# A hybrid mLSTM / gated-delta block on one core: when the z gate jobs enter the instruction streams, and three small moves around them

## The chip, the cores and the metric

The kernel runs on one core of a Trainium2 chip. The metric is the device time of one execution in microseconds (us). TensorE (PE) multiplies, VectorE (DVE) and ScalarE (ACT) do elementwise work, GpSimd (POOL) issues some of the DMAs and does some scaling, and SyncE (SP) issues most of the DMAs.

## The reference

The layer mixes two branches and then applies a feed-forward part, for 256 tokens and 2048 channels, in float32. Cut to what matters here:

```python
h = rms_norm(x, norm_mix_w) * (1 + scale_m) + shift_m
proj = h @ w_in                      # q, k, v, gates of both branches, merge gates
# branch B, 16 heads: gated delta rule; each chunk needs the inverse of a
# unit lower triangular matrix  a_mat = I + beta * (k k^T) * decay
o_b = rms_norm(gated_delta_both_directions(...), gdn_norm_w)
y_b = (o_b * silu(b_z)) @ w_branch_b          # b_z is the "z" gate
x = x + gate_m * ((g_a * y_a + g_b * y_b) @ w_out)     # stage o
hf = rms_norm(x, norm_ffn_w) * (1 + scale_f) + shift_f
x = x + gate_f * ((silu(hf @ w_gate) * (hf @ w_up)) @ w_down)
return rms_norm(x, norm_final_w)
```

## The kernel before

**Jobs.** Nearly every weight matrix is read once, in 1 MB pieces (a tile `raw_*`, loaded by SP). Each piece is cut into two halves, and each half is split into a high part `wh` (ScalarE, a copy that rounds) and a low part `wl` (VectorE, raw minus `wh`, line 211). TensorE then runs three products, high by high, high by low, low by high (lines 230 to 232), so a half of a job made by `tjob` costs 12 matmuls of 128x512. `raw`, `wh` and `wl` have three buffers each, so VectorE can be at most three halves ahead of TensorE. A job is a Python generator that gives out one half per step; the list `fills` holds the waiting jobs, and `fill(n)` takes n steps from its head.

**The 16 heads of branch B.** They go in four groups of four (g = 0 to 3). `gdn_phase1(h)` prepares a head: it ends with VectorE writing the tile `mi` from the product `ks`, and with GpSimd sending 32x32 blocks of `mi` to DRAM (`inst_d`, four DMAs), loading the decay factors `al` of head h+2 (`decay_load`, a memset and a 256 KB broadcast), and reading the blocks back as rows of the tile `uu` (line 657). When the four heads of a group are there, `gdn_invert(g)` solves the triangular blocks in `uu`: a memset (line 684) and 60 short VectorE operations in a chain (lines 689 and 695), and GpSimd stores the result (`inv_d`). `gdn_blocks(g)` loads it back (`cg`) and makes the tile `R`, which the first product of `gdn_phase2`, `p` (line 746), needs. While VectorE solves, `fill` gives TensorE projection jobs. The first of them is `z_job(g + 1)`, the z gate of the next group: four pieces, eight halves, 96 matmuls (`acc_z`).

**What sets the order.** Each engine runs its own queue in order. A scheduler writes the queues from the program, and may move instructions among each other; those wrapped in `order(...)` with a true second argument (or none) keep the program's order. In `tjob`, `early` is both the number of halves prepared before the first matmul and the argument that keeps the job's `wh` and `wl` instructions in program order:

```python
            order(S.activation(wh, raws[u][:, k0 : k0 + 2], AF.Copy), early)
            settle()
            order(V.tensor_tensor(wl, raws[u][:, k0 : k0 + 2], wh.bitcast(F32), ALU.subtract), early)
```

The z job of groups 1 to 3 is made with `early` = 1, near the end of the second `gdn_phase2` of a group.

**Behind stage o.** The last column block of stage o ends in three parts: token tile 0, then the left and right half of token tile 1 (`last_o`). VectorE multiplies by the gate row `gm` (`tm`, line 1199), adds to `x1` (line 1200), ScalarE squares and sums, and from the sums come the two scales `rs1` per token tile. ScalarE, VectorE and GpSimd then scale `x1` to `xn`; TensorE transposes `xn` (`pxn`) and the feed-forward part starts with the job `gt0` (`acc_gt`). GpSimd makes `xn` 1 to 3 (line 1252); `xn` 0 is made by the others.

**The end.** The last sums of stage d are followed by four scalings of 128x512 and four stores per token tile, all issued by SP (line 1416).

Of the kernel before, what the change touches and what calls it, by code (L numbers as in the profile page):

```python
# [11 lines left out]
AF = mybir.ActivationFunctionType  # L12
ALU = mybir.AluOpType
# [4 lines left out]
D = 2048  # L18
# [3 lines left out]
NH_B, DK_B = 16, 128  # L22
# [3 lines left out]
GRP = 4  # L26
# [26 lines left out]
def hybrid_block(ctx: ExitStack, tc: tile.TileContext, xr, nfr, crow, pk_d, cst_d, ada2, ada4, win0, winb, wint, wba, wbb, wo, wgu, wd, out, dbg=None):  # L53
    nc = tc.nc
    V, S, G, PE = nc.vector, nc.scalar, nc.gpsimd, nc.tensor
# [15 lines left out]
    def order(ins, yes=True):  # L71

        return tc.keep_in_program_order(ins) if yes else ins
# [189 lines left out]
    fills = []  # L263
# [34 lines left out]
    heads, parts = {}, {}  # L298
# [11 lines left out]
    def decay_load(h):  # L310
        al = als[h] = fr.tile([P, 2, T + 8], F32, tag="al", bufs=2, name=f"al{h}")
        order(G.memset(al[:, :, 0:8], 0.0))
        order(G.dma_start(al[:, :, 8:], alpha_d[:, h].partition_broadcast(P)))
# [48 lines left out]
    def z_job(g, early=0):  # L362
        def done(ps):
            szs[g] = evp.tile([P, 2, 512], F32, tag="sz", bufs=1, name=f"sz{g}")
            for t in range(2):
                S.activation(szs[g][:, t], ps[t], AF.Silu)
        return tjob(f"z{g}", [wint[g, u] for u in range(4)], hh, hl, done, early)
# [121 lines left out]
    with ExitStack() as s0:  # L489
# [3 lines left out]
        ss = w0.tile([P, 2], F32, name="ssx")  # L493
# [68 lines left out]
        zj = z_job(0, 3)  # L562
# [20 lines left out]
    def gdn_phase1(h):  # L583
# [13 lines left out]
        sq = fr.tile([P, 2, T], F32, tag="sqkq", bufs=1, name=f"sqkq{h}")  # L597
# [48 lines left out]
        g, hl_ = divmod(h, GRP)  # L646
# [5 lines left out]
                inst[4 * b : 4 * b + 4].rearrange("x j i -> j x i"), mi[32 * b : 32 * b + 32, :, 32 * b : 32 * b + 32]  # L652
            ), b)

        if h + 2 < NH_B:
            decay_load(h + 2)
        order(G.dma_start(uus[g][16 * hl_ : 16 * hl_ + 16], inst))

        cc = ccs[h % NB]

# [350 lines left out]
    for g in range(4):  # L1011
        blocks = gdn_blocks(g)
        next(blocks)
        fill(8)
        next(blocks)
        fill(1)
        pairs = [gdn_phase2(g, p) for p in range(2)]
        if g == 3:
            settle()
            sf.close()  # L1020
            mq["pool"] = pool(sq_, "mq", side="right")
            first2 = [mlstm(h) for h in range(2)]
            for c in first2:
                next(c)
        every[0] = (4, 2, 2, 2)[g]
        for p in range(2):
            pieces = stream(4 * g + 2 * p + 4)
            for n in range(1, 10):

                held[0] = n < 4  # L1030
                if p == 0:
                    next(blocks, None)
                if n == 9 and p and g < 3:

                    zj = z_job(g + 1, int(4 * g + 7 in heads))
                    if 4 * g + 7 in heads:
                        next(zj)
                next(pairs[p], None)
                if g == 3 and n == (8, 4)[p]:
                    next(first2[p])  # L1040
                for _ in range(last[n] if g == 3 else second[n] if p else after[n]):
                    next(pieces)
            for _ in pairs[p]:
                pass

            if g < 3:
                while 4 * g + 2 * p + 5 not in heads:
                    next(pieces)
        if g < 3:
            fills.insert(0, zj)  # L1050
            every[0] = owed[0] = 0
            if asked:
                add()
            invert(g + 1)
# [96 lines left out]
    gm = room[0][0].tile([P, D], F32, name="gm")  # L1151
# [38 lines left out]
    wp = pool(sw, "wp")  # L1190
    x1 = xp.tile([P, 2, D], F32, name="x1")
    S.dma_start(x1, xr)

    def residual(t, g, ps, gate, ss, rp, hold=False, part=slice(0, 512), acc=None, new=slice(0, 512)):

        c = slice(g * 512 + part.start, g * 512 + part.stop)
        n = slice(g * 512 + new.start, g * 512 + new.stop)
        tm = rp.tile([P, 512], F32, tag="tm", bufs=2, name=f"tm{ss.name}_{t}_{g}_{part.start}")
        order(V.tensor_tensor(tm[:, part], ps[:, : part.stop - part.start], gate[:, c], ALU.mult), hold)
        order(V.tensor_tensor(x1[:, t, c], x1[:, t, c], tm[:, part], ALU.add), hold)  # L1200
        order(S.activation(tm[:, new], x1[:, t, n], AF.Square, accum_out=ss[:, t, g : g + 1] if acc is None else acc), hold)

# [6 lines left out]
        order(V.tensor_reduce(rs[:, 3:5], ss[:, :, 0:3], mybir.AxisListType.X, ALU.add))  # L1209
        order(V.tensor_scalar(rs[:, 3:5], rs[:, 3:5], 1.0 / D, EPS, ALU.mult, ALU.add))  # L1210

    def token_root(rs, t):

        order(S.activation(rs[:, t : t + 1], rs[:, 5 + t : 6 + t], AF.Sqrt, bias=rs[:, 3 + t : 4 + t], scale=1.0 / D))

    def token_rstd(rs, t):
        order(V.reciprocal(rs[:, t : t + 1], rs[:, t : t + 1]))

    ss1 = xp.tile([P, 2, 4], F32, name="ss1")
    rs1 = xp.tile([P, 8], F32, name="rs1")  # L1220
# [26 lines left out]
    def normed(q, t, parts, eng):  # L1247
        if q not in xns:
            xns[q] = hp.tile([P, 2, 512], F32, tag="sg", bufs=2, name=f"xn{q}")
        o, i = xns[q][:, t, parts], x1[:, t, q * 512 + parts.start : q * 512 + parts.stop]  # L1250
        if eng is G:
            G.tensor_scalar(o, i, rs1[:, t : t + 1], None, ALU.mult)
        elif eng is V:
            order(V.tensor_scalar(o, i, rs1[:, t : t + 1], None, ALU.mult))
        else:
            order(S.activation(o, i, AF.Copy, scale=rs1[:, t : t + 1]))
# [3 lines left out]
    def last_o(t, ps, part):  # L1260

        sq = rs1[:, 5 + t : 6 + t]
        if not t:
            residual(0, 3, ps, gm, ss1, wp, True, acc=sq)
            token_root(rs1, 0)
        elif part == left:
            residual(1, 3, ps, gm, ss1, wp, True, acc=sq, new=left)
            order(V.scalar_tensor_tensor(rs1[:, 4:5], sq, 1.0 / D, rs1[:, 4:5], ALU.mult, ALU.add))
            token_rstd(rs1, 0)
            normed(0, 0, left, S)  # L1270
        else:
            residual(1, 3, ps, gm, ss1, wp, True, part, sq, part)
            token_root(rs1, 1)
            token_rstd(rs1, 1)

    def front_o():
# [73 lines left out]
    normed(0, 1, left, V)  # L1350
    for t in range(2):
        normed(0, t, right, S)
    for b in range(2):
        scaled, high = block(b)
        scaled()
        high()
# [44 lines left out]
    def finish(t):  # L1401

        token_root(rs2, t)
        token_rstd(rs2, t)
        r = rs2[:, t : t + 1]
        for g in (2, 0, 3, 1):
            o = x1[:, t, g * 512 : (g + 1) * 512]
            if g == 3:
                order(V.scalar_tensor_tensor(o, o, r, nf[:, 3 * 512 :], ALU.mult, ALU.mult))
            elif g == 2:  # L1410
                order(V.tensor_scalar(o, o, r, None, ALU.mult))
            else:
                order(S.activation(o, o, AF.Copy, scale=r))
        for g in (2, 0, 3, 1):
            c = slice(g * 512, (g + 1) * 512)
            order(nc.sync.dma_start(out[:, t, c], x1[:, t, c]))

    def front_d():
        means(ss2, rs2)
# [2 lines left out]
    for g in range(4):  # L1422
        c = slice(g * 512, (g + 1) * 512)
# [114 lines left out]
```

## Time and profile before

| | us |
|---|---|
| median of 3 runs (lowest, highest) | 2067.28 (2060.01, 2068.92) |
| the profiled execution | 2064.07 |
| its span, first to last instruction | 2062.1 |
| PE busy in the span | 2019.9 (98%) |
| VectorE busy | 1397.8 (68%) |
| ScalarE busy | 1027.7 (50%) |
| GpSimd busy | 116.8 (6%) |

The span lies 2.0 us under the time of its own execution. In rows of instructions the columns are start, duration, engine, line, operation, output<-inputs, shape and count; a bracket gives the idle time of the engine before the row and what ended it. Equal rows that follow each other are merged, with their count. A start is in us from the span's start. In rows of stretches each engine has its busy time and its count of instructions, then come the granted TensorE clock as a share of full speed, the busy share of the DMA engines and GB/s.

### The profile page before, as it was taken

To read this page: it belongs to the slowest core of one execution; us is meant where nothing else is said; L and a number is where in the kernel's file an instruction comes from. 1 tells how busy PE (TensorE), PEld (TensorE's weight loads), DVE (VectorE), ACT (ScalarE), POOL (GpSimd) and SP (SyncE) were. 2 spreads that over 40 slices of the span, in tenths; PEclk is the share of its full clock that TensorE was granted. 3 is DMA by queue.
4 is the path that set the end of the run, shared out by engine and by line. 5 is a ranking of instruction groups with operands and counts; after the bars stand their busy time and mean duration, and the time that the engine had idled before them with its cause. 6 is when DMAs were issued, how large, how long until landed. Compare 5 with 4: busy or idle time off the path is not lost.

```text
span 2062.1 us, 27024 instructions
## 1 busy us (share of the span) xinstructions
PE 2019.9 (98%) x10386; PEld 1697.9 (82%) x10386; DVE 1397.8 (68%) x2062; ACT 1027.7 (50%) x1540; POOL 116.8 (6%) x211
## 2 busy tenths in 40 slices
PE   8999999999999999999999999999999999999998
PEld 6878789978997889789787888788888888878886
DVE  5778877867878788866577778756565655455554
ACT  3146647755665577454534444644444444444443
POOL 0001210111001010110100000200000000000000
PEclk9999999999999999999999999999999999999999
DMA  9986666646666767586776878466766665555553
GB/s 401 420 334 208 193 228 225 215 124 218 227 206 207 241 213 244 189 291 250 258 278 249 321 283 296 157 232 232 255 225 226 251 237 184 187 201 191 197 189 137
DMA packets 78962, 485.64 MB, mean 236 GB/s; under 512 B 10585, under 2 KB 15969, under 8 KB 24433
## 3 DMA queue, kind: packets, MB, share of 16 engines
q1 hardware_dynamic: 63360, 450.95, 60.4%
q0 software_dynamic: 8160, 17.88, 4.0%
q10 hardware_dynamic: 7314, 15.10, 1.9%
q8 instruction: 81, 1.33, 0.3%
q14 instruction: 47, 0.39, 0.1%
HBM read 467.07 MB, written 16.82 MB: 235 GB/s over the span
## 4 chain that ended last, share of the span: by engine, by line
PE 85%; DMA 6%; DVE 6%; ACT 1%; issue 1%; POOL 0%; ACTq 0%; SPq 0%; DVEq 0%; POOLq 0%
PE acc_gt L230 4%; PE acc_gt L232 4%; PE acc_gt L231 4%; PE acc_up L232 4%; PE acc_up L230 4%; PE acc_up L231 4%; PE acc_d L231 4%; PE acc_d L230 4%; PE acc_d L232 4%; DMA ra<-ada 3%; PE acc_o L230 3%; PE acc_o L232 3%; PE acc_o L231 3%; PE acc_b L187 2%; PE acc_b L188 2%; PE acc_b L189 2%
## 5 line engine op out<-in xcount | busy, mean ns | idle before, releaser
L211 DVE TENSOR_TENSOR wl_d<-raw_d,wh_d 128x1024 fp32r<-128x1024 f32 x88 | 107.8, 1225 | 119.9 <-ACT wh_d L209 119.9
L211 DVE TENSOR_TENSOR wl_up<-raw_up,wh_up 128x1024 fp32r<-128x1024 f32 x88 | 107.7, 1225 | 111.3 <-ACT wh_up L209 111.2
L211 DVE TENSOR_TENSOR wl_gt<-raw_gt,wh_gt 128x1024 fp32r<-128x1024 f32 x88 | 108.1, 1229 | 89.2 <-ACT wh_gt L209 89.2
L187 PE MATMUL acc_b<-hh,wh_b 128*128 128x256 f32 x576 | 164.8, 286 | 0.0
L209 ACT ACTIVATE wh_d<-raw_d 128x1024 fp32r<-128x1024 f32 x88 | 93.3, 1061 | 138.9 <-PE acc_d L231 134.0
L189 PE MATMUL acc_b<-hh,wl_b 128*128 128x256 f32 x576 | 160.9, 279 | 0.0
L188 PE MATMUL acc_b<-hl,wh_b 128*128 128x256 f32 x576 | 159.7, 277 | 0.0
L209 ACT ACTIVATE wh_gt<-raw_gt 128x1024 fp32r<-128x1024 f32 x88 | 93.3, 1060 | 128.7 <-PE acc_gt L231 77.3
L111 DVE SCALAR_TENSOR_TENSOR ada<-ada,crow 128x2048 f32<-128x2048 f32 x64 | 146.1, 2282 | 10.2 <-DMA ada<-ada 10.2
L209 ACT ACTIVATE wh_up<-raw_up 128x1024 fp32r<-128x1024 f32 x88 | 93.2, 1060 | 118.1 <-PE acc_up L231 84.2
L230 PE MATMUL acc_gt<-wh_gt,hfh 128*128 128x512 f32 x352 | 139.0, 395 | 0.0
L231 PE MATMUL acc_gt<-wh_gt,hfl 128*128 128x512 f32 x352 | 138.2, 393 | 0.0
L232 PE MATMUL acc_gt<-wl_gt,hfh 128*128 128x512 f32 x352 | 137.4, 390 | 0.0
L230 PE MATMUL acc_up<-wh_up,hfh 128*128 128x512 f32 x352 | 136.9, 389 | 0.0
L231 PE MATMUL acc_up<-wh_up,hfl 128*128 128x512 f32 x352 | 136.9, 389 | 0.0
L232 PE MATMUL acc_up<-wl_up,hfh 128*128 128x512 f32 x352 | 136.9, 389 | 0.0
L230 PE MATMUL acc_d<-wh_d,ffh 128*128 128x512 f32 x344 | 134.3, 391 | 0.0
L231 PE MATMUL acc_d<-wh_d,ffl 128*128 128x512 f32 x344 | 134.3, 390 | 0.0
L232 PE MATMUL acc_d<-wl_d,ffh 128*128 128x512 f32 x344 | 133.9, 389 | 0.0
L557 PE MATMUL first<-x,raw 128*128 128x256 f32 x512 | 115.9, 386 | 6.3 <-ACT x L551 6.3
L557 PEld LDWEIGHTS first<-x,raw 128*128 128x128 f32 x512 | 97.3, 192 | 25.0 <-ACT x L551 11.9
L187 PEld LDWEIGHTS acc_b<-hh,wh_b 128*128 128x128 f32 x576 | 108.5, 188 | 1.2 <-issue 0.9
(373 smaller groups left out, 5261.3 us busy)
## 6 DMA issues: line engine op xcount, KB each, us to landing
ada<-ada SPq DMA_DIRECT2D x64, 1024.0 KB, 5.0
raw_gt<-wgu SPq DMA_DIRECT2D x44, 1024.0 KB, 4.9
raw_up<-wgu SPq DMA_DIRECT2D x44, 1024.0 KB, 4.9
raw_d<-wd SPq DMA_DIRECT2D x44, 1024.0 KB, 4.8
raw_b<-winb SPq DMA_DIRECT2D x36, 1024.0 KB, 5.1
ra<-ada SPq DMA_DIRECT2D x32, 1025.0 KB, 15.2
raw<-win SPq DMA_DIRECT2D x16, 1024.0 KB, 14.5
raw_z<-wint SPq DMA_DIRECT2D x16, 1024.0 KB, 5.4
```

What stands on the lines that cost most here:

```text
L111: order(V.scalar_tensor_tensor(raw, raw, 1.0, row_c[:, :D], ALU.mult, ALU.mult, accum_out=mod[:, c : c + 1]), room[0][3] > 1)
L187: PE.matmul(o, wh[:, k], hh[:, kk], start=kk == 0, stop=False)
L188: PE.matmul(o, wh[:, k], hl[:, kk], start=False, stop=False)
L189: PE.matmul(o, wl[:, k], hh[:, kk], start=False, stop=kk == KB - 1)
L209: order(S.activation(wh, raws[u][:, k0 : k0 + 2], AF.Copy), early)
L211: order(V.tensor_tensor(wl, raws[u][:, k0 : k0 + 2], wh.bitcast(F32), ALU.subtract), early)
L230: order(PE.matmul(ps[t], xh[:, kk, c], wh[:, k], start=kk == 0, stop=False), early and steps > 1)
L231: PE.matmul(ps[t], xl[:, kk, c], wh[:, k], start=False, stop=False)
L232: PE.matmul(ps[t], xh[:, kk, c], wl[:, k], start=False, stop=kk == last)
L557: PE.matmul(first[o], raw[:, o], x[:, b], start=b == 0 and o % 2 == 0, stop=b == KB - 1 and o % 2 == 1)
```

## The change

Five edits, all shown in the diff:

```diff
-        if h + 2 < NH_B:
+        final = hl_ == GRP - 1
+        if h + 2 < NH_B and not final:
             decay_load(h + 2)
         order(G.dma_start(uus[g][16 * hl_ : 16 * hl_ + 16], inst))
+        if h + 2 < NH_B and final:
+            decay_load(h + 2)
...
-                if n == 9 and p and g < 3:
-
-                    zj = z_job(g + 1, int(4 * g + 7 in heads))
-                    if 4 * g + 7 in heads:
-                        next(zj)
...
-            fills.insert(0, zj)
+            fills.insert(0, z_job(g + 1))
...
-    def residual(t, g, ps, gate, ss, rp, hold=False, part=slice(0, 512), acc=None, new=slice(0, 512)):
+    def residual(t, g, ps, gate, ss, rp, hold=False, part=slice(0, 512), acc=None, new=slice(0, 512), between=None):
...
         order(V.tensor_tensor(tm[:, part], ps[:, : part.stop - part.start], gate[:, c], ALU.mult), hold)
+        if between:
+            between()
         order(V.tensor_tensor(x1[:, t, c], x1[:, t, c], tm[:, part], ALU.add), hold)
...
-            G.tensor_scalar(o, i, rs1[:, t : t + 1], None, ALU.mult)
+            G.tensor_scalar(o, i, ss1[:, t, 3:4], None, ALU.mult)
...
         elif part == left:
             residual(1, 3, ps, gm, ss1, wp, True, acc=sq, new=left)
-            order(V.scalar_tensor_tensor(rs1[:, 4:5], sq, 1.0 / D, rs1[:, 4:5], ALU.mult, ALU.add))
-            token_rstd(rs1, 0)
-            normed(0, 0, left, S)
         else:
-            residual(1, 3, ps, gm, ss1, wp, True, part, sq, part)
-            token_root(rs1, 1)
+            def first_tile():
+                order(V.scalar_tensor_tensor(rs1[:, 4:5], sq, 1.0 / D, rs1[:, 4:5], ALU.mult, ALU.add))
+                token_rstd(rs1, 0)
+                normed(0, 0, left, S)
+
+            residual(1, 3, ps, gm, ss1, wp, True, part, rs1[:, 7:8], part, first_tile)
+            token_root(rs1, 1, 7)
             token_rstd(rs1, 1)
...
+    order(S.activation(ss1[:, :, 3], rs1[:, 0:2], AF.Copy))
...
-            order(nc.sync.dma_start(out[:, t, c], x1[:, t, c]))
+            order((S if t and g == 1 else nc.sync).dma_start(out[:, t, c], x1[:, t, c]))
```

First, for the last head of a group GpSimd issues the load of `uu` ahead of the decay load. Second, the z job of groups 1 to 3 is made at the start of the solve, with `early` = 0, so its `wh` and `wl` instructions are free for the scheduler. Third, behind stage o the product of the last half goes ahead of the two small operations for token tile 0. Fourth, GpSimd takes its scale from a copy that ScalarE writes after its own scalings. Fifth, the very last store is issued by ScalarE.

How the queues move, at three places. VectorE around the solve of group 1, before (`mi7` belongs to the group's last head, `dec8` are scans of the next one):

```order
L645 STREAM_TRANSPOSE mi7_3700<-mb7_3701 128x256
L211 TENSOR_TENSOR wl_z1_0_0_3730<-raw_z1_0_3727,wh_z1_0_0_3729 128x1024
L590 SCALAR_TENSOR_TENSOR dec8_4611<-al8_3487,cst_75 128x256
L591 SCALAR_TENSOR_TENSOR dec8_4611<-al8_3487,cst_75 128x128
L592 SCALAR_TENSOR_TENSOR dec8_4611<-al8_3487,cst_75 128x256
L211 TENSOR_TENSOR wl_z1_0_2_3765<-raw_z1_0_3727,wh_z1_0_2_3764 128x1024
L211 TENSOR_TENSOR wl_z1_1_0_3783<-raw_z1_1_3780,wh_z1_1_0_3782 128x1024
L211 TENSOR_TENSOR wl_z1_1_2_3799<-raw_z1_1_3780,wh_z1_1_2_3798 128x1024
L593 SCALAR_TENSOR_TENSOR dec8_4611<-al8_3487,cst_75 128x128
L684 MEMSET uu1_2779 64x32
```

The same queue now, first what stands ahead of `mi7`:

```order
L211 TENSOR_TENSOR wl_z1_0_0_3743<-raw_z1_0_3740,wh_z1_0_0_3742 128x1024
L613 TENSOR_TENSOR nn7_3691<-sm7_3690 128x2
L843 TENSOR_TENSOR so1_1_5630<-sm6_3454 128x2
L843 TENSOR_TENSOR so1_1_5630<-sm7_3690 128x2
L617 TENSOR_TENSOR sm7_3690<-bT_87,nn7_3691 128x4
L618 TENSOR_SCALAR sm7_3690<-sm7_3690 128x4
L211 TENSOR_TENSOR wl_z1_0_2_3765<-raw_z1_0_3740,wh_z1_0_2_3764 128x1024
L211 TENSOR_TENSOR wl_z1_1_0_3783<-raw_z1_1_3780,wh_z1_1_0_3782 128x1024
L635 SCALAR_TENSOR_TENSOR mi7_3700<-ks7_0_3704,sm7_3690,dec7_3641 128x128
```

Further down the same queue now, from the end of `mi7` to the solve:

```order
L645 STREAM_TRANSPOSE mi7_3700<-mb7_3701 128x256
L590 SCALAR_TENSOR_TENSOR dec8_4611<-al8_3487,cst_75 128x256
L591 SCALAR_TENSOR_TENSOR dec8_4611<-al8_3487,cst_75 128x128
L592 SCALAR_TENSOR_TENSOR dec8_4611<-al8_3487,cst_75 128x256
L211 TENSOR_TENSOR wl_z1_1_2_3799<-raw_z1_1_3780,wh_z1_1_2_3798 128x1024
L593 SCALAR_TENSOR_TENSOR dec8_4611<-al8_3487,cst_75 128x128
L211 TENSOR_TENSOR wl_z1_2_0_3826<-raw_z1_2_3823,wh_z1_2_0_3825 128x1024
L211 TENSOR_TENSOR wl_z1_2_2_3848<-raw_z1_2_3823,wh_z1_2_2_3847 128x1024
L687 MEMSET uu1_2779 64x32
```

Three z halves now stand ahead of `mi7`, and six instead of four ahead of the memset that waits for `uu`. In group 2 four stand ahead of the memset, as before, three of them now ahead of the scans `dec12`; the fifth goes from behind eight operations of the solve to behind four. In group 3 the four ahead of the memset stay, and the fifth goes from behind eight operations to behind one.

ScalarE where the z job of group 3 begins, before (`obt` evicts the transposes `px` of the second `gdn_phase2`, `cc3` are copies of `mi15`):

```order
L621 ACTIVATE vv15_7668<-vps15_7589,nn15_7662 128x128
L209 ACTIVATE wh_z3_0_0_7697<-raw_z3_0_7695 128x1024
L664 ACTIVATE cc3_1163<-mi15_7671 32x2x32
L664 ACTIVATE cc3_1163<-mb15_7672 32x2x32
L664 ACTIVATE cc3_1163<-mi15_7671 32x2x32
L664 ACTIVATE cc3_1163<-mb15_7672 32x2x32
L667 ACTIVATE cc3_1163<-mi15_7671 64x2x64
L667 ACTIVATE cc3_1163<-mb15_7672 64x2x64
L830 ACTIVATE obt10_7711<-px_2_1_7531,pk_74 128x256
L830 ACTIVATE obt11_7714<-px_2_1_7531,pk_74 128x256
```

The same place now:

```order
L621 ACTIVATE vv15_7668<-vps15_7589,nn15_7662 128x128
L833 ACTIVATE obt10_7699<-px_2_1_7531,pk_74 128x256
L833 ACTIVATE obt11_7702<-px_2_1_7531,pk_74 128x256
L834 DMA ob_d2_116<-obt10_7699 128x256
L834 DMA ob_d2_116<-obt11_7702 128x256
L209 ACTIVATE wh_z3_0_0_7711<-raw_z3_0_7709 128x1024
L667 ACTIVATE cc3_1163<-mi15_7671 32x2x32
```

There the two evictions and their two stores moved ahead of the first z half. In groups 1 and 2 the first three `wh` of the z job now stand ahead of the evictions, where before only the first did.

VectorE behind stage o, now:

```order
L1197 TENSOR_TENSOR tmss1_10872_1_3_256_11471<-acc_o3_2_11458,gm_10132 128x256
L1270 SCALAR_TENSOR_TENSOR rs1_10873<-rs1_10873 128x1
L1217 RECIPROCAL rs1_10873<-rs1_10873 128x1
L1200 TENSOR_TENSOR x1_10870<-x1_10870,tmss1_10872_1_3_256_11471 128x256
L1217 RECIPROCAL rs1_10873<-rs1_10873 128x1
```

Before, the first row stood behind the third. TensorE's queue keeps its order but for a few low-part products of z that move by two or three places, and SP's queue loses one store to ScalarE's.

More of the change, by code (lines that the diff above doesn't have):

```diff
@@ L1210, in means, with token_root @@
         order(V.tensor_scalar(rs[:, 3:5], rs[:, 3:5], 1.0 / D, EPS, ALU.mult, ALU.add))
-    def token_root(rs, t):
-        order(S.activation(rs[:, t : t + 1], rs[:, 5 + t : 6 + t], AF.Sqrt, bias=rs[:, 3 + t : 4 + t], scale=1.0 / D))
+    def token_root(rs, t, part=None):
+        order(S.activation(rs[:, t : t + 1], rs[:, part or 5 + t :][:, :1], AF.Sqrt, bias=rs[:, 3 + t : 4 + t], scale=1.0 / D))
     def token_rstd(rs, t):
```

## The prediction

> **What bounds the kernel now.** I read the busy table first, then the waits, then TensorE's stretches around the z jobs, then each engine's rows there.
>
> ```profile
> PE 2019.9 (98%) x10386; PEld 1697.9 (82%) x10386; DVE 1397.8 (68%) x2062; ACT 1027.7 (50%) x1540; POOL 116.8 (6%) x211
> ...
> PE acc_z L232 <- DVE wl_z L211: 9.8, 10, 2.5
> ...
> 441.80:464.00 22.20, 17.77 (x61) 13.69 (x62) 0.00 (x0) 0.85 0.46 126
> 637.50:665.00 27.50, 24.22 (x96) 17.41 (x96) 0.49 (x1) 1.00 0.52 146
> 826.00:852.90 26.90, 23.67 (x96) 17.48 (x96) 0.41 (x1) 1.00 0.43 141
> ...
> 464.03 0.39 PE L231 MATMUL acc_z<-wh_z,hl 128*128 128x512 f32 x1
> 464.26 0.39 PE L232 MATMUL acc_z<-wl_z,hh 128*128 128x512 f32 x1
> ```
>
> TensorE is busy nearly throughout, so only what stops or slows it counts. The largest stop that its own wait list names is the z job waiting for VectorE's low parts. The three stretches hold the z matmuls of groups 1 to 3 (first numbers: length, TensorE busy, count). Undisturbed, one starts every 0.23 us (464.03 to 464.26). So 61 need 14.0 us and took 22.2: group 1 loses 8.2. Group 2 holds 96 and two of the next job, 22.4 in 27.5: it loses 5.1. Group 3 loses 26.9 - 22.0 = 4.9. Together 18.2 us lie there: the ceiling for the z edit.
>
> ```profile
> 444.92 0.73 PE L232 MATMUL acc_z<-wl_z,hh 128*128 128x512 f32 x2 [1.90 <-DVE wl_z L211]
> 459.82 0.60 PE L232 MATMUL acc_z<-wl_z,hh 128*128 128x512 f32 x1 [2.49 <-DVE wl_z L211]
> ...
> 446.30:449.80 3.50, 3.50 (x10) 2.69 (x9) 3.50 (x5) 1.30 (x2) 1.21 (x3) 0.52 0.59 54
> 459.80:463.30 3.50, 3.48 (x9) 2.70 (x10) 3.29 (x9) 0.00 (x0) 0.00 (x0) 0.54 0.00 0
> ...
> 440.83 0.35 DVE L635 SCALAR_TENSOR_TENSOR mi<-ks,sm,dec 128x128 f32<-128x128 f32 x1 [4.44 <-PE ks L630]
> 443.68 1.18 DVE L211 TENSOR_TENSOR wl_z<-raw_z,wh_z 128x1024 fp32r<-128x1024 f32 x1
> 446.28 3.47 DVE L211 TENSOR_TENSOR wl_z<-raw_z,wh_z 128x1024 fp32r<-128x1024 f32 x3
> 456.60 0.17 DVE L689 TENSOR_TENSOR utmp<-uu 64x30 f32<-64x30 f32 x1 [6.52 <-issue]
> ```
>
> Group 1's 8.2 us are two stops, 1.90 and 2.49, and after each some 3.5 us at a granted clock of 0.52 and 0.54 (the clock is the third number from the end), about 1.7 us lost each time. Both stops come from order: the first `wl` stands behind `mi7`, before which VectorE sat idle for 4.44 us; the fifth stands behind the memset that waits for `uu`, before which it sat idle for 6.52.
>
> **The z edit, group 1.** Three `wl` now run in the 4.44 us hole; nothing but buffers holds them. The first stop goes. Each `wl` is 1.16 us (3.47 for three); the third needs the buffer that TensorE frees just before `ks`, so it can push `mi7`, and with it the load of `uu`, later by 0 to 1.2 us. I take 1.1. Six halves are ready before the memset: six times 12 matmuls are 16.5 us, which carry TensorE from its start at 441.8 to 458.3. The solve must have passed its first five operations by then.
>
> ```profile
> 444.05 2.18 POOL L651 DMA_DIRECT2D inst_d<-mi  x4 [16.92 <-DVE mi L645]
> 447.97 0.52 POOL L657 DMA_DIRECT2D uu<-inst_d  x1 [0.97 <-DMA inst_d<-mi]
> ...
> DMA to landing us min/median/max: 2.0/4.4/8.7
> ...
> 832.07 0.51 POOL L657 DMA_DIRECT2D uu<-inst_d  x1 [1.95 <-DMA inst_d<-mi]
> 837.57 0.19 DVE L689 TENSOR_TENSOR utmp<-uu 64x30 f32<-64x30 f32 x1 [3.55 <-DMA uu<-inst_d]
> ...
> 456.50:491.60 35.10, 32.61 (x136) 26.31 (x135) 33.23 (x74) 16.75 (x18) 2.24 (x4) 0.95 0.53 180
> ```
>
> **The decay load.** The load of `uu` goes out at 447.97, after waiting 0.97 for the `inst_d` blocks, so removing the decay load ahead of it hardly brings its issue forward. What it removes is 256 KB of traffic in front. Group 3's last head has no decay load: there `uu` goes out at 832.07 and the solve begins at 837.57, 5.5 us. In group 1 it was 447.97 to 456.60, 8.6. Bounds for the new time are 2.0 and 8.7, the fastest and slowest landing of these loads (2.0/4.4/8.7 above); I take 5.4, near the row of the same place. With 1.1 of delay the solve begins at 454.5, between 451 and 458. The delayed decay load serves a head much later and costs nothing; its cover is the whole solve.
>
> Now VectorE becomes the limit: over a solve it is busy 33.23 of 35.10 us. Starting 2.1 us earlier with one half fewer inside (1.2), the solve keeps pace with TensorE but for some stops of under 1 us. Of 8.2 I take 6.8; bounds 4.5 and 8.2.
>
> **Group 2 and 3.**
>
> ```profile
> 641.76 0.50 PE L230 MATMUL acc_z<-wh_z,hh 128*128 128x512 f32 x1 [0.87 <-ACT wh_z L209]
> 651.69 0.51 PE L230 MATMUL acc_z<-wh_z,hh 128*128 128x512 f32 x1 [0.84 <-ACT wh_z L209]
> 648.26 0.19 DVE L689 TENSOR_TENSOR utmp<-uu 64x30 f32<-64x30 f32 x1 [3.03 <-issue]
> ...
> 825.39 0.60 PE L826 MATMUL px<-cst,on 128*128 128x128 f32 x4
> 828.82 0.73 PE L232 MATMUL acc_z<-wl_z,hh 128*128 128x512 f32 x2 [1.60 <-DVE wl_z L211]
> 840.83 0.51 PE L232 MATMUL acc_z<-wl_z,hh 128*128 128x512 f32 x1 [0.96 <-DVE wl_z L211]
> 824.92 1.05 ACT L209 ACTIVATE wh_z<-raw_z 128x1024 fp32r<-128x1024 f32 x1
> 828.07 0.84 ACT L830 ACTIVATE obt<-px,pk 128x256 f32<-128x256 f32 x2
> ```
>
> Group 2: the stop at 641.76 (second `wh` behind the evictions) goes, since it now stands ahead of them; the piece whose late arrival stops TensorE at 651.69 reuses a buffer that VectorE frees about 3 us earlier, so that goes as well. The first low part still follows `mi11`: 0.8 us stay. The solve can start 1 to 3 us before 648.26, and VectorE then limits the middle. Of 5.1 I take 3.0; bounds 1 and 4.3.
>
> Group 3: the first `wl` stays behind `mi15`, so the 1.60 stays; worse, the first `wh` now waits for `px` (825.39) and two evictions (0.84) with their stores. It ran at 824.92; it would end near 828.2, and its `wl` near 829.4, so TensorE resumes about 0.6 later than at 828.82, after standing for 2.2 us. In these rows 1.60 kept the clock and 1.90 lost it, so I charge the 1.7 us. The later stops (0.96 and three of some 0.3) go with the fifth half no longer behind eight operations: with the smaller waits between, 3.3. So 3.3 - 0.6 - 1.7 = 1.0; bounds -1.5 and 2.7.
>
> [...]
>
> **Behind o.**
>
> ```profile
> 1310.87 0.41 DVE L1199 TENSOR_TENSOR tmss<-acc_o,gm 128x256 f32<-128x256 f32 x1
> 1311.31 0.87 DVE L1200 TENSOR_TENSOR x<-x,tmss 128x256 f32<-128x256 f32 x1
> 1311.22 1.57 POOL L1252 TENSOR_SCALAR xn<-x,rs 128x512 f32<-128x512 f32 x1 [247.54 <-DVE rs L1217]
> 1313.02 0.89 ACT L1256 ACTIVATE xn<-x,rs 128x256 f32<-128x256 f32 x2
> 1313.75 1.75 PE L1318 MATMUL pxn<-cst,xn 128*128 128x128 f32 x7 [1.81 <-DVE xn L1254]
> ```
>
> The product (0.41) can run at 1310.2, in the hole before the two small operations, so the addition starts at about 1311.0 instead of 1311.31. It took 0.87 while GpSimd's scaling ran, against 0.41 for a product of the same shape; with GpSimd behind ScalarE's copy it should take 0.4. ScalarE's square follows at about 1311.5, once its own scaling is done. Gain 0.8, bounds 0 (the ScalarE scaling in between moves later too) and 1.3. ScalarE's copy of two columns adds some 0.2 us, on an engine that waits there. GpSimd starts about 2 us later; its `xn` 1 is needed at 1319, and two scalings of 1.6 to 2.2 end by 1317.7.
>
> [...]
>
> **The last store.**
>
> ```profile
> 2056.22 1.33 ACT L1413 ACTIVATE x<-x,rs 128x512 f32<-128x512 f32 x2 [0.23 <-DVE rs L1217]
> 2056.74 1.80 SPq L1416 DMA_DIRECT2D outT<-x  x4
> DMA to landing us min/median/max: 2.0/2.4/2.7
> ```
>
> ScalarE ends the last block at 2057.55; SP's four issues, 0.45 each, begin the last at 2058.1. ScalarE can issue at 2057.6. Gain 0.4, bounds -0.3 (these stores land after 2.0 to 2.7 us, and the last may land at the slow end) and 0.5.
>
> **Sum.** 6.8 + 3.0 + 1.0 + 0.8 + 0.4 = 12.0 us. The profiled time of 2064.07 becomes 2052.1. That execution lies 3.2 under the median shown; the mean of all four times is 2065.1, and less 12.0 that is 2053, which I give.
>
> **Rivals.** (1) VectorE as the bound: the gain at the starts of the z jobs is handed back within the solves. For it speaks 33.23 of 35.10; against it, in group 1, that six halves stand ahead of the wait and one half fewer lies inside the solve. If `uu` lands as late as before, group 1 keeps 4.5 and group 2 1.5, group 3 loses 0.5, and the last two edits bring 1: 6.5 us, which is 2058.5 from the mean of 2065.1. (2) Full recovery: `uu` lands in 2 to 4 us, the clock holds in group 3: 8.2 + 4.3 + 2.7 + 1.7, 17 us, 2048. (3) The z edit does not do what it says: stops of the same size reappear one half later. The order speaks against it, since six halves stand ahead of the wait; only the tails remain, 1 us, 2064. (4) Slower: the solve of group 1 comes too late for `R`.
>
> ```profile
> 505.97 0.71 DVE L710 STREAM_TRANSPOSE cg<-cg 128x512 f32<-128x512 f32 x1 [1.42 <-DMA cg<-inv_d]
> 513.49 0.97 PE L746 MATMUL p<-R,cc 128*128 128x32 f32 x8
> ```
>
> `cg` came at 505.97 and `R`'s first half some 1.5 us later, 6 us before `p` at 513.49. With the stops gone TensorE reaches `p` at 506 or so, while `cg` comes 2 to 3 us earlier: still in time. It turns into a loss if the solve starts over 6 us later than at 456.6, which means a `uu` load of over 8.7 + 6 less the 1 us of delay, about 14 us; the longest was 8.7. Each us beyond is lost: at 24 us in one group 10 are lost, with the low-clock 1.7 behind the stop, less the 1 us of the last two edits: 2076.
>
> **Chances.** My forecast (gain 9 to 15) 0.55, rival 1 0.27, rival 2 0.09, rival 3 0.06, rival 4 0.03. A measurement of this kernel tells about 0.5% from no change, 10.3 us, so 2056.9 parts faster from same. Faster takes most of the forecast (0.5), rival 2 and a little of rival 1 (0.03): 0.62. Slower takes rival 4: 0.03. The rest, 0.35, is same. The range reaches from rival 2 to between rivals 1 and 3: 2047 to 2062; the runs before spread over 9 us, so I widen it to 2046 to 2063.
>
> **What would show it.** Right: no TensorE stop over 0.9 us in group 1's z job and full clock there; `utmp` starting 4 to 6 us after the `uu` issue; a first z matmul of group 3 late by about 2 us; the addition behind o near 0.4 us. Wrong: new TensorE waits for `wl` inside the solves, or a `p` that waits for `R`.

## The result, and the profile after

| us | before | after |
|---|---|---|
| median of the runs (lowest, highest) | 2067.28 (2060.01, 2068.92) | 2052.43 (2050.61, 2056.26) |
| ratio to before, 95% interval | | 0.9939 (0.9926, 0.9953) |
| span of the profiled execution | 2062.1 | 2054.3 |

The ratio is 12.6 us (9.7 to 15.3) of 2067.28. The profiled executions lie only 7.8 us apart: the one shown of after is the longest of its runs, and the one shown of before lies 3.2 us under the median. So the change is read from stretches that hold the same matmuls. The busy line, and of TensorE's waits of after the row that answers to the 9.8 us shown of before (waited for: us in total, times, longest; in both kernels 1.1 of it lies in group 0):

```profile
PE 2017.2 (98%) x10386; PEld 1698.6 (83%) x10386; DVE 1397.7 (68%) x2062; ACT 1027.4 (50%) x1541; POOL 116.6 (6%) x211
...
PE acc_z L232 <- DVE wl_z L211: 3.0, 2, 2.0
```

Next the stretches of the three z jobs with the work around them, from the start of the same first to the start of the same last matmul (282, 192 and 223 of them; the counts in the rows take in those that overlap a bound). First before, then after. The first number after the bounds is the length, the next TensorE's busy time, the third from the end the granted clock.

```profile
434.07:506.06 71.99, 67.60 (x284) 54.10 (x284) 50.41 (x109) 32.60 (x42) 9.92 (x19) 0.95 0.54 178
628.13:676.21 48.08, 45.13 (x193) 34.35 (x192) 39.84 (x93) 25.75 (x35) 5.72 (x11) 1.00 0.67 222
818.02:861.10 43.08, 39.84 (x225) 32.52 (x224) 31.75 (x74) 24.45 (x35) 4.90 (x9) 1.00 0.51 175
```

```profile
433.81:497.66 63.85, 63.85 (x285) 51.97 (x284) 50.27 (x108) 32.15 (x42) 9.94 (x19) 1.00 0.62 201
621.11:667.55 46.44, 43.97 (x193) 34.66 (x192) 38.38 (x89) 25.64 (x35) 5.74 (x11) 1.00 0.63 217
810.50:852.92 42.42, 39.91 (x226) 34.21 (x224) 32.04 (x75) 24.57 (x35) 4.91 (x9) 0.96 0.51 175
```

Group 1 saves 8.14 us and has no idle TensorE left (63.85 of 63.85) and full clock. Group 2 saves 1.64, group 3 0.66, there at a clock of 0.96. The rows behind these numbers, of after: GpSimd's load of `uu`, the first operation of the solve, the same two of group 2 with its one large stop and the fifth high part, and the start of group 3; below them the stretch behind that last stop (TensorE's columns alone: length, busy, count, clock, DMA).

```profile
448.86 0.51 POOL L658 DMA_DIRECT2D uu<-inst_d  x1 [1.74 <-DMA inst_d<-mi]
453.44 0.19 DVE L692 TENSOR_TENSOR utmp<-uu 64x30 f32<-64x30 f32 x1 [1.23 <-DMA uu<-inst_d]
...
636.78 0.52 POOL L658 DMA_DIRECT2D uu<-inst_d  x1 [3.71 <-DMA inst_d<-mi]
638.60 2.01 ACT L209 ACTIVATE wh_z<-raw_z 128x1024 fp32r<-128x1024 f32 x2 [3.38 <-DMA raw_z<-wint]
642.40 0.19 DVE L692 TENSOR_TENSOR utmp<-uu 64x30 f32<-64x30 f32 x1 [5.48 <-issue]
644.51 0.50 PE L232 MATMUL acc_z<-wl_z,hh 128*128 128x512 f32 x1 [1.95 <-DVE wl_z L211]
...
821.11 0.53 PE L230 MATMUL acc_z<-wh_z,hh 128*128 128x512 f32 x1 [2.51 <-ACT wh_z L209]
```

```profile
821.42:824.83 3.41, 3.41 (x9) 0.50 0.11 19
```

In group 1 `uu` is in use 4.6 us after its issue (8.6 before). In group 2 the fifth half came late. Its piece was not what held it: ScalarE began its high part at 638.60. Its low part stands behind four operations of the solve, and the solve began at 642.40, since the load of `uu` had waited 3.71 us for the blocks of `inst_d` and was in use 5.6 us after its issue. In group 3 the first z half waits behind the evictions, TensorE stands for 2.51 us and then runs 3.41 us at half clock.

Behind stage o, of after: the product, the addition, the last matmul of o and the first of the feed-forward part. Below them the last two of before.

```profile
1303.15 0.42 DVE L1197 TENSOR_TENSOR tmss<-acc_o,gm 128x256 f32<-128x256 f32 x1
1303.79 0.41 DVE L1200 TENSOR_TENSOR x<-x,tmss 128x256 f32<-128x256 f32 x1
...
1302.76 0.28 PE L255 MATMUL acc_o<-wl_o,mgh 128*128 128x256 f32 x1
1307.41 0.79 PE L230 MATMUL acc_gt<-wh_gt,hfh 128*128 128x512 f32 x1
```

```profile
1309.85 0.28 PE L255 MATMUL acc_o<-wl_o,mgh 128*128 128x256 f32 x1
1315.46 0.80 PE L230 MATMUL acc_gt<-wh_gt,hfh 128*128 128x512 f32 x1
```

5.61 us became 4.65: 0.96 saved, with the first feed-forward matmuls at half clock in both. At the end, ScalarE's last scalings and its store of after; then the 3 us behind ScalarE's last scaling in after, and the same of before (the last two numbers are the busy share of the DMA engines and GB/s):

```profile
2048.39 1.33 ACT L1417 ACTIVATE x<-x,rs 128x512 f32<-128x512 f32 x2 [0.23 <-DVE rs L1217]
2049.75 0.36 ACTq L1420 DMA_DIRECT2D outT<-x  x1
```

```profile
2049.70:2052.70 3.00, 0.00 (x0) 0.00 (x0) 0.00 (x0) 0.03 (x1) 0.00 (x0) 0.50 0.93 350
```

```profile
2057.50:2060.50 3.00, 0.00 (x0) 0.00 (x0) 0.00 (x0) 0.06 (x1) 0.00 (x0) 0.50 0.91 350
```

ScalarE ends at 2049.72 and the span at 2054.26: 4.54 us. Before it was 2057.56 to 2062.10: 4.54 as well.

### The profile page after: what moved, and what is told of

Its sections match the earlier page's. It is cut to its first block, busy times and chain, and to the rows that moved or that the text cites. A ratio compares the mean times of both kernels' runs of the same rounds, so it can differ in the third digit from the quotient of the medians.

```text
span 2054.3 us, 27025 instructions
## 1 busy us (share of the span) xinstructions
PE 2017.2 (98%) x10386; PEld 1698.6 (83%) x10386; DVE 1397.7 (68%) x2062; ACT 1027.4 (50%) x1541; POOL 116.6 (6%) x211
## 4 chain that ended last, share of the span: by engine, by line
PE 86%; DMA 6%; DVE 5%; ACT 1%; issue 1%; POOL 0%; ACTq 0%; SPq 0%; DVEq 0%; POOLq 0%
PE acc_gt L230 4%; PE acc_gt L232 4%; PE acc_gt L231 4%; PE acc_up L232 4%; PE acc_up L231 4%; PE acc_up L230 4%; PE acc_d L230 4%; PE acc_d L232 4%; PE acc_d L231 4%; DMA ra<-ada 3%; PE acc_o L232 3%; PE acc_o L230 3%; PE acc_o L231 3%; PE acc_b L187 2%; PE acc_b L188 2%; PE acc_b L189 2%
## 5 line engine op out<-in xcount | busy, mean ns | idle before, releaser
L209 ACT ACTIVATE wh_gt<-raw_gt 128x1024 fp32r<-128x1024 f32 x88 | 93.3, 1060 | 128.7 <-PE acc_gt L231 77.3
L209 ACT ACTIVATE wh_up<-raw_up 128x1024 fp32r<-128x1024 f32 x88 | 93.2, 1060 | 118.0 <-PE acc_up L231 84.2
## 6 DMA issues: line engine op xcount, KB each, us to landing
ra<-ada SPq DMA_DIRECT2D x32, 1025.0 KB, 15.3
```

## The experiments

What the profile left open: whether the z edit or the load of `uu` carries group 1; whether the late first half costs group 3 what it looks like; which part of the work behind o brings the 0.96; and why stops of like length sometimes halve the clock.

**One edit at a time: `z_only`, `uu_first`, `tails`.** Each is the kernel before with a part of the diff above.

```diff
# z_only
-                if n == 9 and p and g < 3:
-                    zj = z_job(g + 1, int(4 * g + 7 in heads))
-                    if 4 * g + 7 in heads:
-                        next(zj)
-            fills.insert(0, zj)
+            fills.insert(0, z_job(g + 1))
# uu_first
-        if h + 2 < NH_B:
+        final = hl_ == GRP - 1
+        if h + 2 < NH_B and not final:
             decay_load(h + 2)
         order(G.dma_start(uus[g][16 * hl_ : 16 * hl_ + 16], inst))
+        if h + 2 < NH_B and final:
+            decay_load(h + 2)
# tails: the third, fourth and fifth edit of the change
```

> The kernel before with the second edit alone: the z jobs of groups 1 to 3 are made at the start of the solve, their halves free to move. My theory (the places of the z halves carry the gain, the order of the uu load adds to it): both stops of group 1 named in the prediction go, but uu still lands about 8.6 us after its issue, so the seventh half, behind five operations of the solve, comes 1 to 2 us late in group 1. Gain 5 to 6.6 us there, about 1.7 in group 2, 0.4 in group 3: 7 to 9 us in all, ratio 0.9957 to 0.9966. Rival A (the uu load carries the second stop): a stop of over 2 us with its low clock stays, gain about 5 us, ratio 0.9976. Rival B (the z edit does it all): 11 us or more, ratio 0.9945 or less, no TensorE stop over 0.9 us in group 1.

> The kernel before with the first edit alone: for the last head of a group GpSimd issues the uu load ahead of the decay load; no other engine's order moves. My theory: uu lands in about 4.6 us instead of 8.6 in group 1, so the second stop of group 1 (2.49 us with 1.7 of low clock) goes and the first (1.90) stays; group 2 gains 0 to 2 us, group 3 nothing, since its last head has no decay load. 4 to 6 us in all, ratio 0.997 to 0.998. Rival (the memset and the decay traffic were hidden, the landing depends on other traffic): landing still about 8 us, stop stays, ratio 0.9995 or more.

> The kernel before with the three edits behind the heads alone (product first behind stage o, GpSimd's scaling later, last store on ScalarE's queue). My theory from the two profiles: the addition takes 0.4 us instead of 0.87 and the first feed-forward matmul comes 0.6 to 0.8 us earlier relative to the last matmul of stage o; the last store brings nothing, from ScalarE's last scaling to the end 4.5 us as before. 0.6 to 0.8 us in all, ratio 0.9996, not to be told from 1 by the clock. Rival (the prediction): the store brings 0.4 more, 4.1 us from the last scaling to the end. [...]

Measured: `z_only` 0.9965 (0.9951, 0.9978), `uu_first` 0.9971 (0.9962, 0.9981), `tails` 0.9995 (0.9986, 1.0004). Group 1 of each, in that order:

```profile
433.59:500.01 66.42, 64.73 (x284) 51.51 (x284) 50.26 (x108) 32.13 (x42) 9.95 (x19) 1.00 0.60 194
```

```profile
433.25:501.40 68.15, 65.54 (x284) 51.48 (x284) 50.22 (x108) 32.60 (x42) 9.97 (x19) 1.00 0.58 188
```

```profile
433.64:505.45 71.81, 66.83 (x285) 52.70 (x284) 50.57 (x109) 32.59 (x42) 9.95 (x19) 0.98 0.56 179
```

And the solve's first operation after the issue of `uu`, of `z_only` (with its one stop in group 1) and then of `uu_first`:

```profile
448.65 0.52 POOL L657 DMA_DIRECT2D uu<-inst_d  x1 [0.98 <-DMA inst_d<-mi]
456.15 0.17 DVE L689 TENSOR_TENSOR utmp<-uu 64x30 f32<-64x30 f32 x1 [4.16 <-issue]
471.69 0.50 PE L232 MATMUL acc_mb<-wl_mb,hh 128*128 128x512 f32 x1 [1.69 <-DVE wl_mb L211]
```

```profile
447.17 0.52 POOL L658 DMA_DIRECT2D uu<-inst_d  x1 [1.74 <-DMA inst_d<-mi]
452.21 0.20 DVE L692 TENSOR_TENSOR utmp<-uu 64x30 f32<-64x30 f32 x1 [2.94 <-DMA uu<-inst_d]
```

The z edit alone saves 5.57 in group 1, the load's order alone 3.84, together 8.14. Alone they add up to 1.3 us more than together. Both act on the second stop, 2.49 us before: it is gone in `z_only` and 0.23 in `uu_first`. How much they overlap there is not shown: the first stop of `uu_first`, still 1.91 us, kept full clock by where it fell (below), while before lost some 1.7 us behind it, so up to 1.7 of the 3.84 need not come of the load. Rival A and rival B of the first expectation both fall: each edit carries a part. The late half that I expected in `z_only` came later, in the job behind the z job, with 1.69 us. The load's order does what it was priced for: from issue to use 5.0 us in `uu_first` against 8.6 before, and 4.6 in the changed kernel against 7.5 in `z_only`, which differs from it there in the decay load alone. The three ratios multiply to 0.9931, near the measured 0.9939. In `tails` the way from the last matmul of o to the first of the feed-forward part is 4.64 us, all of the 0.96, and the end takes 4.53 us from ScalarE's last scaling: the store brings nothing.

**Group 3's late first half: `z3_before`, `z3_free`, `z_all_free`.** The first puts the z job of group 3 back to its old place. The second does too, but leaves its instructions free to move. The third does this for all groups.

```diff
# z3_before
+                if n == 9 and p and g == 2:
+                    zj = z_job(g + 1, int(4 * g + 7 in heads))
+                    if 4 * g + 7 in heads:
+                        next(zj)
-            fills.insert(0, z_job(g + 1))
+            fills.insert(0, zj if g == 2 else z_job(g + 1))
# z3_free: this, and in tjob for the z jobs (fixed=False)
-            order(S.activation(wh, ...), early)
+            order(S.activation(wh, ...), early and fixed)
-            order(V.tensor_tensor(wl, ...), early)
+            order(V.tensor_tensor(wl, ...), early and fixed)
# z_all_free: as z3_free, with g < 3 in the first line and zj for every group
```

> The changed kernel, but the z job of group 3 is made where the kernel before made it, so in group 3 the first z half stands ahead of the obt evictions again, and the fifth behind eight operations of the solve. My theory: the TensorE stop of 2.5 us at the start of group 3 shrinks to about 1.6, the stops at the fifth half (1.0 and some of 0.3) come back; against the changed kernel between 0.5 us slower and 2 us faster, ratio 0.993 to 0.994. Rival (the delayed first half costs nothing, the load of raw or the px transposes set the start): the first stop stays at about 2.5 us and the kernel is 1 to 2 us slower than the changed one, ratio 0.9945.

> The changed kernel, but the first half of group 3's z job is taken where the kernel before took it, and its instructions stay free to move: the first high part stands ahead of the obt evictions as before, the fifth low part ahead of the memset. My theory (the late first half is what the changed kernel loses in group 3): the first TensorE stop of group 3 is 1.6 us (or less) instead of 2.5, mostly without half clock, and the stops at the fifth half stay away; the stretch of group 3 is 1 to 2.6 us shorter than in the changed kernel, ratio to before 0.9925 to 0.9935. Rival (the time before the solve is fixed by mi15 and its blocks, a stop moved is a stop found again in the solve): the stretch of group 3 stays within 0.5 us of the changed kernel's.

> As the run beside it, for groups 2 and 3 (in group 1 the queues come out as in the changed kernel): the high parts of group 2's first halves also stand six places further ahead of the obt evictions. My theory: group 2 as in the changed kernel (1.6 to 4.6 us shorter than before, by when the pieces land), group 3 as in the run beside it. Rival (high parts taken early keep buffers from the job that runs then): group 2's stretch longer than in the changed kernel, with a stop in the job ahead of it.

Measured: 0.9949 (0.9936, 0.9961), 0.9930 (0.9918, 0.9942) and 0.9937 (0.9923, 0.9951). Group 3 of the three in this order, with the first stop of `z3_free` in the second fence:

```profile
808.85:852.12 43.27, 39.99 (x225) 32.64 (x224) 31.84 (x74) 24.45 (x35) 4.92 (x9) 1.00 0.51 173
```

```profile
807.59:849.07 41.48, 38.84 (x225) 32.75 (x224) 30.85 (x73) 24.48 (x35) 4.93 (x9) 1.00 0.51 177
...
818.52 0.73 PE L232 MATMUL acc_z<-wl_z,hh 128*128 128x512 f32 x2 [1.61 <-DVE wl_z L211]
```

```profile
805.96:846.91 40.95, 38.82 (x225) 32.73 (x224) 30.82 (x73) 24.46 (x35) 4.91 (x9) 1.00 0.51 180
```

With the old place and order (43.27) nothing of group 3's gain is left: 0.85 us slower than after, where I had expected between 0.5 slower and 2 faster. The first stop is 1.59 us again, as expected, and the stops at the later halves are back: 0.81, 0.23, 0.32 and 0.28. With the old place but a free order (41.48) both are had: a first stop of 1.61 and none later. That is 0.9 us shorter than after's 42.42, just short of the 1 to 2.6 that I expected, and `z_all_free` (40.95) is 1.5 shorter; its group 2, at 44.32, lies between the two of the changed kernel (46.44 and, below, 44.03). By the times measured the three kernels and the changed one cannot be told apart: their intervals overlap.

**A second profile and the rest: `after_again`, `fill5`, `gpsimd_early`, `store_sp`.**

```diff
# fill5
-        fill(4 if g else 6)
+        fill((6, 4, 5, 4)[g])
# gpsimd_early
-            G.tensor_scalar(o, i, ss1[:, t, 3:4], None, ALU.mult)
+            G.tensor_scalar(o, i, rs1[:, t : t + 1], None, ALU.mult)
-    order(S.activation(ss1[:, :, 3], rs1[:, 0:2], AF.Copy))
# store_sp
-            order((S if t and g == 1 else nc.sync).dma_start(out[:, t, c], x1[:, t, c]))
+            order(nc.sync.dma_start(out[:, t, c], x1[:, t, c]))
```

> The changed kernel once more, for a second profile and for a comparison on the chip of the next run. My theory: no TensorE stop over 0.9 us in group 1, a stop of about 2.5 us at the start of group 3, the 2 us stop in group 2 present or not (it hangs on when inst_d and raw_z land), ratio 0.993 to 0.995. Rival (the gain was in the half-clock stretches of one chip): ratio 0.997 or more.

> The changed kernel with one number more: in the program five halves instead of four are taken ahead of the memset of group 2's solve, which in the queues puts the fifth low part of group 2 ahead of that memset and, since every later half comes one step earlier, two high parts of group 3 ahead of the obt evictions. My theory: the stop at the fifth half of group 2 (1.95 us) goes whenever the pieces land, and the start of group 3 loses 1.6 us at most instead of 2.5 with its low clock: 1 to 4 us faster than the changed kernel, ratio to before 0.992 to 0.9935. Rival (the memset now waits for a low part whose piece lands late, and the solve of group 2 with it): no gain over the changed kernel, or a loss of up to 2 us, with a stop at p or in the solve.

> The changed kernel with the fourth edit undone: GpSimd scales from the sums' own column again, as soon as VectorE has the scale. My theory: the addition behind stage o takes 0.87 us again instead of 0.41, since GpSimd's scaling runs beside it, and the first feed-forward matmul comes about 0.4 us later: half of the 0.83 us gained behind o. Rival (only the order of the product counts): addition at 0.4, all 0.83 us kept. [...]

> The changed kernel with the last store issued by SP again. My theory: the four last stores move 1 MB at one rate from the first packet, so the end does not hang on who issues the last: 4.5 us from ScalarE's last scaling to the end, as in both kernels. Rival (the prediction): 0.3 to 0.5 us longer.

`after_again` measured 0.9938 (0.9924, 0.9952), with a span of 2047.9: the same kernel again, without the 1.95 stop. Its groups 2 and 3, and the first operation of the solve of group 2:

```profile
621.20:665.23 44.03, 43.69 (x194) 34.74 (x192) 38.53 (x89) 25.77 (x35) 5.74 (x11) 1.00 0.68 229
807.84:850.10 42.26, 39.75 (x226) 34.16 (x225) 32.05 (x75) 24.58 (x35) 4.91 (x9) 0.96 0.51 175
...
638.47 0.19 DVE L692 TENSOR_TENSOR utmp<-uu 64x30 f32<-64x30 f32 x1 [1.31 <-issue]
```

So group 2's saving varies from one execution to the next: 1.64 and 4.05 in two of the same kernel. ScalarE began the fifth high part at nearly the same time in both (638.60 and 638.26); the solve began at 642.40 in one and at 638.47 in the other. Before is not one number either: `tails`, whose queues in group 2 are those of before, took 49.25 us there against 48.08.

`fill5` measured 0.9936 (0.9920, 0.9952), no gain over the changed kernel. In group 2 the stop at the fifth half is gone, and 43.49 us are 0.5 less than the better of the changed kernel's two; then a job step that came earlier does harm:

```profile
622.81:666.30 43.49, 43.41 (x194) 34.82 (x192) 38.21 (x89) 25.53 (x35) 5.74 (x11) 1.00 0.70 236
...
752.30 1.06 ACT L209 ACTIVATE wh_o<-raw_o 128x1024 fp32r<-128x1024 f32 x1 [7.61 <-DMA raw_o<-wint]
753.26 0.40 ACT L337 ACTIVATE vf<-cv 128x256 f32<-128x256 f32 x1
753.72 0.44 PE L601 MATMUL vps<-cst,vf 128*128 128x128 f32 x2 [3.56 <-ACT vf L337]
754.48:761.31 6.83, 6.83 (x20) 0.50 0.10 40
```

Group 2 saves 4.6, and a stop of 3.56 us with 6.83 us at half clock (3.4 lost) hands 7 back at 754, more than it had gained on the changed kernel. (Its group 3 holds other matmuls and is not compared; the first z stop there is 0.36.) The rows show why: with every later half one step earlier, one `wh_o` more stands ahead of `vf` in ScalarE's queue (23 of them, 22 in after). It waited 7.61 us for its piece, `vf` waited behind it, and TensorE waited for `vf`. Neither theory had this.

`gpsimd_early`, one execution (2053.38 us). GpSimd scales early again, yet the addition keeps its 0.41, since it now ends when GpSimd has only begun:

```profile
1299.54 0.41 DVE L1200 TENSOR_TENSOR x<-x,tmss 128x256 f32<-128x256 f32 x1
1299.89 3.14 POOL L1252 TENSOR_SCALAR xn<-x,rs 128x512 f32<-128x512 f32 x2 [250.24 <-DVE rs L1217]
...
1298.52 0.28 PE L255 MATMUL acc_o<-wl_o,mgh 128*128 128x256 f32 x1
1303.38 0.80 PE L230 MATMUL acc_gt<-wh_gt,hfh 128*128 128x512 f32 x1
```

From o to the feed-forward part it takes 4.86 us: the order of the product alone brings 0.75 of the 0.96. For GpSimd's later start at most 0.2 is left, and that is not shown: the nine traces with both edits lie between 4.64 and 4.79. My expectation of a half each was wrong.

`store_sp`, one execution (2051.37 us): 4.55 us from ScalarE's last scaling to the end with the store on SP's queue, against 4.54 with it on ScalarE's.

**Why some stops halve the clock: `pden_apart`.** In all traces the half-clock stretches begin a multiple of 3.41 us apart, as in a grid that runs through: in before at 446.42, 460.08, 569.30, 995.97 and 1313.41, which are 4, 32, 125 and 93 steps apart. I laid each trace's grid over TensorE's rows; a cell is one step of the grid. Cells with 2.3 us or more without a matmul: 23 up to then, all followed by a half-clock cell. Cells with 1.89 to 1.98: 8, of which 6. Cells with 1.0 to 1.7: 49, of which 4, all with the cell ahead idle for over 1.4 as well. Unexplained were the cells near 985 and 1060 us, where TensorE has no gap but runs 24 matmuls of one column. After, near 985:

```profile
985.71 2.73 PE L950 MATMUL pden<-ones,mdec 128*128 128x1 f32 x24
...
985.31:988.72 3.41, 3.41 (x29) 1.00 0.85 259
988.72:992.14 3.42, 3.42 (x10) 0.50 0.45 169
```

```diff
# pden_apart: z3_free, and in mlstm(h)
+        if h % 2:
+            yield
         pd_ = gps(f"pden{h}")
```

> The kernel of the run z3_free, and in branch A the denominators of the second head of a pair are multiplied one step later, so that the 24 one-column matmuls pden, 2.7 us in one go, come as two lots of 12 with wide matmuls between. A test of what halves the clock: in all traces so far the clock halved near 985 us or near 1060 us behind these lots, although TensorE's rows show it busy there. My theory (a stretch of 3.41 us is judged by how much of it wide matmuls fill; one-column matmuls count as idle): with 1.4 us at a time no stretch near 985 or 1060 us halves the clock; 1.7 to 3.4 us faster than z3_free, ratio to before 0.9915 to 0.9925. Rival (the half clock there comes of something else): a half-clock stretch near 985 or 1060 us as before, ratio 0.993 or more, since the second head's chain now ends later.

```profile
980.50 1.39 PE L952 MATMUL pden<-ones,mdec 128*128 128x1 f32 x12
...
975.00:1090.00 115.00, 113.53 (x502) 1.00 0.76 267
```

With lots of 12 no half clock is left there, for the first time in 13 traces. The time does not tell it: 0.9934 (0.9915, 0.9954), no gain over `z3_free` (0.9930) that could be measured. In the clock column my theory held (1.00 over these 115 us, 0.99 over the same bounds in `z3_free`); a gain of 1.7 to 3.4 us is not shown. The 24 lots of 24 in the other 12 traces say the same: if they are counted as idle, 14 of them fell so that one cell had 2.0 us or more idle, and half clock followed all 14; ten were split so that no cell had more than 1.86, and it followed none.

## Why the prediction was right, point by point

The sum was 12.0 us, the measured ratio 12.6 (9.7 to 15.3), and 2053.0 was forecast against 2052.43. By terms, with the same stretches:

| term | predicted (bounds) | measured |
|---|---|---|
| group 1 | 6.8 (4.5 to 8.2) | 8.14 in the change's trace and all others with both edits |
| group 2 | 3.0 (1 to 4.3) | 1.64 and 4.05; 2.3 to 4.6 in other kernels with the same queues there |
| group 3 | 1.0 (-1.5 to 2.7) | 0.66 and 0.82 |
| behind o | 0.8 (0 to 1.3) | 0.96 (0.82 to 0.97 in the nine traces with both edits there) |
| last store | 0.4 (-0.3 to 0.5) | 0.0 |

In the trace of after the terms add up to 11.4 us, of which the spans show 7.8: the rest went outside these stretches, in half-clock cells among others (two in a row at 558 us, where before has one at 569, and one at 1067, where before has none). In `after_again` they add up to 13.9, and the spans lie 14.2 apart. The misses of the terms partly cancel, and the runs of the changed kernel spread over 5.65 us: that the forecast came within 0.6 us of the median is luck.

**Group 1.** The mechanism held: three low parts in the hole ahead of `mi7`, six halves ahead of the wait, no stop, full clock. Mis-sized was the remainder of 1.4 us that I left for stops inside the solve. There are none: TensorE is busy for 63.85 of 63.85 us. With that rival 1, VectorE as the bound, is out in group 1; its condition, a `uu` as late as before, did not come either. The step on the landing held: 5.4 us forecast, 4.6 measured, and the two pairs that differ in it show that the decay load ahead was the cause (8.6 against 5.0 and 7.5 against 4.6). Its lower bound was misread: the row of 2.0 to 8.7 us takes in 32 stores out of `uu` as well, and the 16 loads of `uu` alone took 3.6 to 8.7 before, so the 2 us of rival 2 had no row.

**Group 2.** The forecast lies in the middle of what one kernel gives in different executions. The step that did not hold is the earlier solve: I let it begin 1 to 3 us earlier, and from the start of the stretch it began after 21.3 us in after and 17.3 in `after_again`, against 20.1 before. In after it stood behind the blocks of `inst_d` (3.71 us of waiting) and the load of `uu` (in use 5.6 us after its issue), and the fifth low part stood behind it. So the middle was hit in part by luck. The 1.95 us in after are also the one sign of being wrong that showed: a new wait for `wl` inside a solve, in one of two executions.

**Group 3.** As argued: the first half waits behind the evictions (2.51 against the 2.2 forecast), half clock behind it, later stops gone, a small gain. The reason I gave for the half clock was too simple. I read 1.60 and 1.90 as the two sides of a length that decides. In `uu_first` the same first stop of group 1 fell across two cells of the grid and kept full clock:

```profile
443.00:446.41 3.41, 1.51 (x7) 1.00 0.31 91
446.41:449.83 3.42, 3.42 (x10) 0.50 0.58 53
```

```profile
444.10 0.73 PE L232 MATMUL acc_z<-wl_z,hh 128*128 128x512 f32 x2 [1.91 <-DVE wl_z L211]
442.61:446.02 3.41, 1.92 (x8) 1.00 0.33 93
446.02:449.44 3.42, 3.38 (x15) 1.00 0.46 152
```

The first fence is of before (stop 1.90 in one cell, busy 1.51), the second of `uu_first` (1.91, of which 1.5 in one cell, busy 1.92). So the length of the stop alone did not tell the two apart; the idle time of one cell, 1.90 against 1.5 us, did. The 2.51 us of group 3 cost the clock in the four traces where they lay in one cell (after, `after_again`, `z_only`, `store_sp`) and not in `gpsimd_early`, where they were split and the cells had 1.90 and 0.67 us idle; that kernel's group 3, with the same queues, took 41.26 us. With 1.90 idle in one cell the clock was halved in before and kept there, so that figure decides nothing by itself.

**Behind o.** The size was right, the cause partly not. I gave the addition's 0.4 us to GpSimd's later start; in `gpsimd_early` the earlier product alone took the addition out of GpSimd's way (0.41 us, ended at 1299.95, with GpSimd beginning at 1299.89). The 0.96 holds up to the first feed-forward matmul. Up to the 96th of `acc_gt`, 25 us further on, 0.46 to 0.75 are left in eight of the nine traces with both edits, and in `tails` 0.17 are lost: its half-clock cell began 5.5 us behind the last matmul of o, in full work, and that of after 3.4 us behind it, partly in the wait.

**Last store.** This step failed. I took the last issue for what sets the end. The issue did come earlier, but the four last stores moved their 1 MB in one stretch (0.91 and 0.93 busy, 350 GB/s over 3 us in the two kernels, and no traffic in the 0.5 us before), and the end came 4.54 us after ScalarE in both, 4.55 in `store_sp`.

Rivals 3 and 4 did not come: no stop of group 1 appeared one half later, and no `p` waited for `R`.

## What to carry to other kernels

Where one engine's queue mixes a chain that waits for a DMA with the feeding of TensorE, put as many feeds ahead of the wait as TensorE needs for the whole wait. Two edits that act on the same wait need not add up: here 9.4 us one at a time and 8.1 together. Before a store or a load is moved to another queue, see whether the DMA engines are idle at that moment: here, with them 0.91 to 0.93 busy, the earlier issue of the last store brought nothing (4.54 us to the end either way). A job step taken early moves the later steps of its list as well: see what each of them now stands ahead of, as the `wh_o` in `fill5` that waited 7.6 us for its piece with `vf` behind it.

## What the hardware showed that I had not expected

In each trace the half-clock stretches begin on one grid of 3.41 us, wherever the kernel's work lies on it. Take the cells of all 13 traces that begin between 30 and 2030 us, and count one-column matmuls as idle. Of cells at full clock, all 41 with 2.0 us or more idle were followed by half clock (in after 2.46, 2.51, 2.43, 2.22 and 2.47 us, in before 2.49, 2.01 and 2.96), 6 of 9 with 1.86 to 1.98, 1 of 3 with 1.7 to 1.85, and of 84 with 1.0 to 1.7 one, behind a cell that was idle for 1.49. Of the cells at half clock, all 10 with 0.63 us or more idle were followed by another (0.83 in before, 1.36 in after), and one of 50 with 0.42 or less. These are counts of this case's traces, and no run shows what lies behind them. With 1.7 us lost in each half-clock cell, an estimate (half of 3.41), a stop of 2 us cost 2, 3.7 or, with two such cells in a row, 5.4 us, by where it fell and by what followed.

A matmul of one column, 0.11 us each in rows that show TensorE busy (2.73 us for 24), is taken as idle here: without that the cells near 985 and 1060 us have no idle time at all (in after 0.0 instead of 2.43 and 2.22). 24 in one go were followed by half clock where one cell held enough of them, in 14 of 24 cases, and 12 (1.39 us) in none of four.
